# A two-stage transformer block on one core: the first modulation's shift and scale computed by TensorE instead of VectorE

## The chip, the cores and the metric

The kernel runs as one program on one core of a Trainium2 chip. The metric is device time in microseconds from one launch. Three runs of the kernel before gave 3837.38, 3837.87 and 3838.32 us, median 3837.87 us. The engines are PE (TensorE), DVE (VectorE), ACT (ScalarE), POOL (GpSimd) and SP (SyncE, which here only issues transfers). Each runs its own list of instructions in order.

## The reference, cut to what matters

The first lines of the reference make a layer norm of the input, a SiLU of the conditioning vector c, and from it the modulation vectors of every sub-layer. The input of the first feed-forward layer is the normed input, scaled and shifted:

```python
x = layer_norm(x, ln_in_g, ln_in_b)
c_act = jax.nn.silu(c)                       # 1 x 1024
for l in range(DEPTH):
    mod = (c_act @ ada_w[l] + ada_b[l]).reshape(b, N_SUB, 3, 1, D_MODEL)
    h = modulate(x, mod[:, 0, 0], mod[:, 0, 1])   # x * (1 + scale) + shift
    y = swiglu_ffn(h, ffn1_w_in[l], ffn1_w_out[l])
    ...
```

The shift and the scale of the very first `modulate` are two products of a vector of 1024 with a 1024 x 1024 matrix. They stand at the start of the program: no token can enter the first feed-forward layer before its shift and scale are there.

## The kernel before, in words

Everything is float32. Weights and activations are split into a high and a low float32r half (`hi`, `lo`; `hh`, `hl`), and each product is three matmuls (hi.hi, hi.lo, lo.hi: lines 347 to 349). Tokens lie 128 to a partition block (`z`, four blocks of 128 tokens x 1024 features, two blocks in each of two tiles); activations for the matmuls lie with features on the partitions, in eight blocks j = 0 to 7 of 128 features (`h`).

`first_norm` (lines 482 to 531) is the start. DVE sums the rows of z, ACT squares them with an accumulated sum (line 561), DVE and POOL make the reciprocal root, DVE normalizes z in place (line 571, four instructions). Then, for each feature block j, DVE multiplies two fetched weight blocks of 128 x 1024 by the row of SiLU(c), which lies replicated on all partitions (`crow`), with the sum accumulated into one column: one instruction for the shift (line 517), one for the scale (line 518). Four small DVE instructions (lines 519 to 522) fold in the biases and the norm's own gain and bias into `md_in`. PE transposes the block of z (line 525, four 128 x 128 transposes), ACT applies scale and bias on the way out of PSUM (line 528, into `sg` or `gf`) and writes the high half `hh` (line 529), DVE writes the low half `hl` (line 530).

The first chunk of the first feed-forward layer follows directly: gate and up products into the PSUM tiles `pgu`, with 256 tokens at a time, 216 matmuls. They read `hh` and `hl` of the feature blocks in turn, so they start while later blocks are still being made.

All weights come over one transfer queue that SP issues in order: the input, the constant columns `cols`, the 16 blocks of the first modulation (`arawf`, 512 KB each, in a pool of four tiles of two blocks), the first feed-forward weights (`raw`), and blocks of later modulations (`araw`), which DVE multiplies in the same way beside the matmuls (line 463). `gb` holds rows that DVE needs to form the next residual base (lines 594 and 596), also at the start.

The program is written in one order and a scheduler places the instructions on each engine's list by its own timing model, so a change in `first_norm` also moves neighbours that the diff does not touch.

Of the kernel before, what the change touches and what calls it, by code (L numbers as in the profile page):

```python
# [10 lines left out]
F32 = mybir.dt.float32  # L11
F32R = mybir.dt.float32r
AF = mybir.ActivationFunctionType
ALU = mybir.AluOpType
# [3 lines left out]
P = 128  # L18
DM = 1024
KT = DM // P  # L20
# [35 lines left out]
def in_blocks(w):  # L56

    k, m = w.shape
    return w.reshape(k // P, P, m // P, P).transpose(2, 1, 0, 3).reshape(m // P, P, k)
# [65 lines left out]
def mla_uq(w):  # L125
    a, b = [], []
    for g in range(4):
        c = w[:, g * 384 : g * 384 + 384]
        a.append(tok_blocks(c[:256], 2)[0])
        b.append(c[256:])  # L130
    return np.stack(a), np.stack(b)
# [13 lines left out]
def ada_blocks(w):  # L145

    d, _, m = w.shape
    return w.reshape(d, DM, m // DM, KT, P).transpose(0, 2, 3, 4, 1)


def feat(x):
    return x.T.reshape(-1, P, x.shape[0])


def tok(x):

    return x.reshape(-1, 2, P, DM).transpose(0, 2, 1, 3).reshape(-1, P, 2 * DM)


def norm_rows(i):  # L160

    r = [(i["ln_in_g"], i["ln_in_b"])]
    r += [(i["ln_g"][l, s], i["ln_b"][l, s]) for l in range(DEPTH) for s in range(3)]
    r += [(i["ln_g_2"][l, s], i["ln_b_2"][l, s]) for l in range(DEPTH) for s in range(2)]
    r = np.array(r, dtype=np.float32)
    return np.broadcast_to(r[:, :, None], (len(r), 2, P, DM))
# [47 lines left out]

def pack(i):
    c = Cols()
    c.vec("ln_in_g", i["ln_in_g"])
    c.vec("ln_in_b", i["ln_in_b"])
    for l in range(DEPTH):
        for s in range(3):  # L220
            c.vec(f"ln_g{l}{s}", i["ln_g"][l, s])
            c.vec(f"ln_b{l}{s}", i["ln_b"][l, s])
        for s in range(2):
            c.vec(f"ln2_g{l}{s}", i["ln_g_2"][l, s])
            c.vec(f"ln2_b{l}{s}", i["ln_b_2"][l, s])
        c.vec(f"ada_b{l}", i["ada_b"][l])
        c.vec(f"ada2_b{l}", i["b_ada_2"][l])
        for k in range(4):
            c.vec(f"conv_w{l}{k}", i["ssd_conv_w"][l, k])
        c.vec(f"conv_b{l}", i["ssd_conv_b"][l])  # L230
        for k in range(3):
            c.vec(f"sconv_w{l}{k}", i["sconv_w"][l, k])
        c.vec(f"norm_g{l}", i["ssd_norm_g"][l])
        c.vec(f"d{l}", np.repeat(i["ssd_d"][l], 64))
        c.row(f"dtf_b{l}", np.concatenate([i["ssd_dt_bias"][l], i["fox_f_bias"][l]]))
        c.row(f"a_log{l}", i["ssd_a_log"][l])
    c.vec("mla_qg", i["mla_q_norm_2"][0])
    c.vec("mla_kvg", i["mla_kv_norm_2"][0])
    consts, coff = shape_consts()
    uqa, uqb = mla_uq(i["mla_w_uq_2"][0])  # L240
    m_in = i["mla_w_in_2"][0]
    arrays = {
        "x": tok(i["x"][0]),
        "ctx": tok(i["ctx_2"][0]),
        "rows": norm_rows(i),
        "gqa_g": np.broadcast_to(np.concatenate([np.tile(i["gqa_q_norm_2"][0], 4), i["gqa_k_norm_2"][0]]), (P, 320)),
        "ctxT": feat(i["ctx_2"][0]),
        "cols": np.concatenate(c.parts, axis=1),
        "crow": np.stack([np.broadcast_to(v, (P, DM)) for v in (i["c"][0], i["c_2"][0], i["c_ctx_2"])]),
        "consts": consts,  # L250
        "ada": ada_blocks(i["ada_w"]),
        "ada2": ada_blocks(i["w_ada_2"]),
        "f1i": np.stack([ffn_in(w) for w in i["ffn1_w_in"]]),
        "f1o": np.stack([ffn_out(w) for w in i["ffn1_w_out"]]),
        "f2i": np.stack([ffn_in(w) for w in i["ffn2_w_in"]]),
        "f2o": np.stack([ffn_out(w) for w in i["ffn2_w_out"]]),
        "mi": np.stack([mix_in(w) for w in i["mix_w_in"]]),
        "mdt": np.stack([mix_dtf(w) for w in i["mix_w_in"]]),
        "mo": np.stack([mix_out(w) for w in i["mix_w_out"]]),
        "qkv": gqa_in(i["gqa_w_qkv_2"][0]),  # L260
        "gwo": chunks_out(i["gqa_w_o_2"][0]),
        "mcq": tok_blocks(m_in[:, :384], 2),
        "mck": tok_blocks(m_in[:, 384:], KT)[0],
        "uqa": uqa,
        "uqb": uqb,
        "ukv": mla_ukv(i["mla_w_ukv_2"][0]),
        "mwo": chunks_out(i["mla_w_o_2"][0]),
        "w1": np.stack([in_blocks(w) for w in i["mlp_w1_2"]]),
        "w2": np.stack([chunks_out(w) for w in i["mlp_w2_2"]]),
    }  # L270
    return {k: np.ascontiguousarray(v) for k, v in arrays.items()}, c.off, coff
# [40 lines left out]
class Kernel:  # L312
# [171 lines left out]
    def first_norm(self, z, g, b, src, bias):  # L484

        nc, fp = self.nc, self.fpool
        tt, stt, ts = nc.vector.tensor_tensor, nc.vector.scalar_tensor_tensor, nc.vector.tensor_scalar  # L490
        T = lambda tag: fp.tile([P, SEQ], F32, tag=tag, bufs=2, name=tag)
        row = self.vector(0)
        h = self.quads(2, SEQ, "h")
        raw = []

        def fetch(j):
            raw.append(fp.tile([P, 2, DM], F32, tag="q4", bufs=4, name="arawf"))
            for i in range(2):
                nc.sync.dma_start(raw[j][:, i], src[i][j])

        for j in range(4):
            fetch(j)
        md = self.cpool.tile([P, 2, KT], F32, name="md_in")
        acc = self.cpool.tile([P, 3, KT], F32, name="acc_in")
        hs, hb = (md[:, i] for i in range(2))
        sums = self.cpool.tile([P, NTB, 2], F32, name="sums_in")
        for tb in range(NTB):
            for n in range(2):
                x = z[tb // 2][:, tb % 2, n * SEQ : (n + 1) * SEQ]
                nc.vector.tensor_reduce(sums[:, tb, n : n + 1], x, axis=AX, op=ALU.add)  # L510
        self.normalize(z, sums, range(NTB), 1e-5)
        for j in range(KT):
            if j >= 4:
                fetch(j)
            c = lambda x: x[:, j : j + 1]
            m = self.apool.tile([P, DM], F32, tag="amul", bufs=1, name="amul")
            stt(m, raw[j][:, 0], 1.0, row, op0=ALU.mult, op1=ALU.mult, accum_out=c(acc[:, 0]))
            stt(m, raw[j][:, 1], 1.0, row, op0=ALU.mult, op1=ALU.mult, accum_out=c(acc[:, 2]))
            ts(c(acc[:, 2]), c(acc[:, 2]), c(bias[1]), 1.0, op0=ALU.add, op1=ALU.add)
            tt(c(acc[:, 1]), c(acc[:, 0]), c(bias[0]), op=ALU.add)  # L520
            tt(c(hs), c(g), c(acc[:, 2]), op=ALU.mult)
            stt(c(hb), c(b), c(acc[:, 2]), c(acc[:, 1]), op0=ALU.mult, op1=ALU.add)
            pt = self.ps("cd"[j % 2], [P, NTB, P], "pth")
            for tb in range(NTB):
                nc.tensor.transpose(pt[:, tb], z[tb // 2][:, tb % 2, j * P : (j + 1) * P], self.ident)
            hf = T(("sg", "gf")[j % 2])
            hh, hl = (x[:, j % 4] for x in h[j // 4])
            nc.scalar.activation(hf, pt.rearrange("p a e -> p (a e)"), AF.Identity, bias=c(hb), scale=c(hs))
            nc.scalar.copy(hh, hf)
            self.base = tt(hl, hf, hh.bitcast(F32), op=ALU.subtract)  # L530
        return h
# [1123 lines left out]
    def run(self):  # L1655
        nc, tc, d = self.nc, self.tc, self.d
        with ExitStack() as es:
# [8 lines left out]
            z = self.load_rows(d["x"], "z")  # L1666
# [91 lines left out]

            phase("start", True)
            g, b = self.col("ln_in_g", KT), self.col("ln_in_b", KT)  # L1760
            h = self.first_norm(z, g, b, (d["ada"][0, 0], d["ada"][0, 1]), [self.col("ada_b0", KT, i * KT) for i in range(2)])
            later(ada1, 0, 0, (2,))
            for l in range(DEPTH):
                m1 = lambda s, j: mod1[:, l * 9 + s * 3 + j]
# [10 lines left out]
                h = norm(z, self.sums[0], SEQ, 1 + l * 3, m1(1, 0), m1(1, 1), 1e-5, f"md{l}0")  # L1775
                phase(f"mix.{l}", False)
                old, z, kept = z, [], []
# [25 lines left out]
                h = norm(z, self.sums[0], SEQ, 2 + l * 3, m1(2, 0), m1(2, 1), 1e-5, f"md{l}1")  # L1803
# [11 lines left out]
                if l == 0:  # L1815
                    h = norm(z, self.sums[0], SEQ, 3, mod1[:, 9], mod1[:, 10], 1e-5, f"md{l}2")
# [5 lines left out]
            h = norm(z, self.sums[0], SEQ, 6, mod2[:, 0], mod2[:, 1], 1e-5, "md12")  # L1822
            for l in range(DEPTH):
                m2 = lambda j: mod2[:, l * 6 + j]
                kept = keep(z)
                src = self.mla_latents(h, hc) if l else (h, hc, self.gqa_first(hc))
                phase(f"attn.{l}", False)
                z, zc = [], []
# [35 lines left out]
                h = norm(z, sums[-1], SEQ, 7 + 2 * l, m2(3), m2(4), 1e-6, f"me{l}0")  # L1864
                parts = [(h, z, m2(5), SEQ), *more]
                self.mlp(parts, self.base_rows(7 + 2 * l))
                if l == 0:
                    sums = self.sums
                    h = norm(z, sums[0], SEQ, 8, mod2[:, 6], mod2[:, 7], 1e-6, f"me{l}1")
# [30 lines left out]
```

## Time and profile before

| | us |
|---|---|
| median of three runs | 3837.87 |
| profiled execution, its own time | 3839.17 |
| its span, first to last instruction | 3837.3 |
| PE busy | 3637.5 (95%) |
| DVE busy | 2529.1 (66%) |
| ACT busy | 1534.4 (40%) |

A row of the page or of a view gives a line of the kernel, an engine, an operation and its tiles as out<-in. In a view by stretches each engine's busy time stands with its number of instructions, then the granted TensorE clock (1.00 is full speed), the mean busy share of the 16 DMA engines and what they moved. "PEld" is the loading of a matmul's stationary operand. A row of the timeline that stands for several instructions (x8) gives the time from the first's start to the last's end. The granted clock reads 1.00 in the first stretches of this trace, ahead of its first record; there the distance between matmuls shows the level.

### The profile page before, as it was taken

To read this page: it belongs to the slowest core of one execution; us is meant where nothing else is said; L and a number is where in the kernel's file an instruction comes from. 1 tells how busy PE (TensorE), PEld (TensorE's weight loads), DVE (VectorE), ACT (ScalarE), POOL (GpSimd) and SP (SyncE) were. 2 spreads that over 40 slices of the span, in tenths; PEclk is the share of its full clock that TensorE was granted. 3 is DMA by queue.
4 is the path that set the end of the run, shared out by engine and by line. 5 is a ranking of instruction groups with operands and counts; after the bars stand their busy time and mean duration, and the time that the engine had idled before them with its cause. 6 is when DMAs were issued, how large, how long until landed. Compare 5 with 4: busy or idle time off the path is not lost. (4 is left out here: it accounts for less than half of the span.)

```text
span 3837.3 us, 49056 instructions
## 1 busy us (share of the span) xinstructions
PE 3637.5 (95%) x18970; PEld 3077.3 (80%) x18970; DVE 2529.1 (66%) x4245; ACT 1534.4 (40%) x2748; POOL 359.3 (9%) x388
## 2 busy tenths in 40 slices
PE   6999999999999999999998898999999979989998
PEld 5888777888888887778887787788888878878887
DVE  8775665777777966579665778664444558776454
ACT  3222443422332234452224566443232457644333
POOL 0000323000000004310001115100000001130000
PEclk9999999999999999999999899999999989999999
DMA  7663322566446633235642001122221210112222
GB/s 289 213 195 119 106 71 99 167 206 208 158 160 198 208 105 111 71 122 186 208 154 72 21 23 67 35 61 66 66 62 55 77 37 30 41 55 91 95 94 66
DMA packets 121738, 428.77 MB, mean 112 GB/s; under 512 B 13656, under 2 KB 19672, under 8 KB 119072
## 3 DMA queue, kind: packets, MB, share of 16 engines
q1 hardware_dynamic: 119584, 421.44, 33.7%
q10 hardware_dynamic: 1920, 4.19, 0.3%
q8 instruction: 149, 2.44, 0.3%
q14 instruction: 85, 0.70, 0.1%
HBM read 415.10 MB, written 10.49 MB: 111 GB/s over the span
## 5 line engine op out<-in xcount | busy, mean ns | idle before, releaser
L296 ACT CAST hi<-raw 128x1024 fp32r<-128x1024 f32 (+2 forms) x502 | 518.4, 1035 | 1314.4 <-PE pgu L348 726.6
L301 DVE TENSOR_TENSOR lo<-raw,hi 128x1024 fp32r<-128x1024 f32 (+2 forms) x472 | 577.0, 1224 | 337.5 <-ACT hi L296 333.8
L348 PE MATMUL pgu<-hl,hi 128*128 128x512 f32 (+1 forms) x1536 | 567.7, 370 | 4.5 <-DVE hl L530 2.9
L347 PE MATMUL pgu<-hh,hi 128*128 128x512 f32 (+1 forms) x1536 | 565.8, 370 | 5.7 <-ACT hh L621 3.3
L349 PE MATMUL pgu<-hh,lo 128*128 128x512 f32 (+1 forms) x1536 | 566.4, 369 | 0.0
L652 DVE TENSOR_TENSOR po<-po,gate 128x512 f32<-128x512 f32 x376 | 259.0, 696 | 357.6 <-PE po L349 357.6
L347 PE MATMUL po<-hi,gh 128*128 128x512 f32 x1216 | 474.4, 391 | 5.6 <-DVE z L654 3.1
L348 PE MATMUL po<-lo,gh 128*128 128x512 f32 x1216 | 472.8, 390 | 0.0
L349 PE MATMUL po<-hi,gl 128*128 128x512 f32 x1216 | 468.0, 389 | 0.0
L463 DVE SCALAR_TENSOR_TENSOR amul<-araw,crow 128x1024 f32<-128x1024 f32 x288 | 351.4, 1220 | 31.5 <-DMA araw<-in_ada 30.1
L348 PEld LDWEIGHTS pgu<-hl,hi 128*128 128x128 f32 x1536 | 292.8, 191 | 54.0 <-DVE hl L530 3.5
L347 PEld LDWEIGHTS pgu<-hh,hi 128*128 128x128 f32 x1536 | 291.4, 191 | 54.2 <-ACT hh L621 3.7
L349 PEld LDWEIGHTS pgu<-hh,lo 128*128 128x128 f32 x1536 | 292.9, 191 | 47.6 <-DVE lo L301 0.3
L347 PEld LDWEIGHTS po<-hi,gh 128*128 128x128 f32 x1216 | 228.4, 188 | 55.3 <-DVE z L654 5.6
L349 PEld LDWEIGHTS po<-hi,gl 128*128 128x128 f32 x1216 | 228.2, 188 | 47.8
L348 PEld LDWEIGHTS po<-lo,gh 128*128 128x128 f32 x1216 | 228.5, 188 | 45.1
L564 POOL TENSOR_TENSOR st<-st,mhalf 128x2 f32<-128x2 f32 (+2 forms) x24 | 19.9, 828 | 2601.9 <-DVE st L563 2601.9
L348 PE MATMUL pm<-hl,hi 128*128 128x512 f32 (+1 forms) x576 | 210.2, 366 | 2.0 <-DVE hl L622 2.0
L347 PE MATMUL pm<-hh,hi 128*128 128x512 f32 (+1 forms) x576 | 210.3, 367 | 1.9 <-ACT hh L621 1.6
L654 DVE TENSOR_TENSOR z<-po,z 128x512 f32<-128x512 f32 x304 | 206.5, 687 | 5.1
L349 PE MATMUL pm<-hh,lo 128*128 128x512 f32 (+1 forms) x576 | 209.5, 364 | 0.2 <-DVE lo L301 0.2
L333 DVE TENSOR_TENSOR gl<-gf,gh 128x512 fp32r<-128x512 f32 (+1 forms) x158 | 105.3, 668 | 115.7 <-ACT gh L331 115.0
(468 smaller groups left out, 7090.9 us busy)
## 6 DMA issues: line engine op xcount, KB each, us to landing
araw<-in_ada SPq DMA_DIRECT2D x224, 512.0 KB, 4.4
raw<-in_w SPq DMA_DIRECT2D x128, 512.0 KB, 3.5
raw<-in_f1i SPq DMA_DIRECT2D x88, 512.0 KB, 4.2
raw<-in_f2i SPq DMA_DIRECT2D x88, 512.0 KB, 3.8
raw<-in_mi SPq DMA_DIRECT2D x48, 512.0 KB, 3.5
raw<-in_f1o SPq DMA_DIRECT2D x44, 512.0 KB, 4.2
raw<-in_f2o SPq DMA_DIRECT2D x44, 512.0 KB, 4.4
arawf<-in_ada SPq DMA_DIRECT2D x16, 512.0 KB, 9.0
```

What stands on the lines that cost most here:

```text
L296: nc.scalar.copy(hi[:, :n], raw[:, :n])
L301: self.lo = nc.vector.tensor_tensor(lo[:, :n], raw[:, :n], hi[:, :n].bitcast(F32), op=ALU.subtract)
L333: ins = eng.tensor_tensor(lo, src, hi.bitcast(F32), op=ALU.subtract)
L347: mm(ps, ah, bh, start=start and i == 0, stop=False)
L348: mm(ps, ah, bl, start=False, stop=False)
L349: mm(ps, al, bh, start=False, stop=stop and i == n - 1)
L463: ins = nc.vector.scalar_tensor_tensor(m, w, 1.0, row, op0=ALU.mult, op1=ALU.mult, accum_out=res[:, j : j + 1])
L564: nc.gpsimd.tensor_tensor(r, sq, self.mhalf[:, :n], op=ALU.pow)
L652: nc.vector.tensor_tensor(ps, ps, gate[:, f], op=ALU.mult)
L654: nc.vector.tensor_tensor(to, ps, zf, op=ALU.add)
```

## The change

The 16 weight blocks are laid out anew ahead of the launch, with the input features on the partitions (`ada_in`), and c becomes one more set of eight columns in `cols`. The transfers are as many and as large as before. ACT makes SiLU(c) of a 128 x 8 column tile `c_in`. For each feature block j and each of shift and scale, PE does eight float32 matmuls: a 128 x 128 piece of the weights is the stationary operand, one column of `c_in` is the moving one, and they accumulate into one column of the PSUM tile `pmd`. That is 128 matmuls. After every second block DVE folds in biases, gain and bias, two columns at a time, in five small instructions. The transposes and what follows them stand in a loop of their own. The long DVE instructions of lines 517 and 518 are gone. The replicated row `crow` is still loaded, for the later modulations.

```diff
 def pack(i):
     c = Cols()
+    c.vec("c", i["c"][0])
...
+        "ada_in": in_blocks(i["ada_w"][0][:, : 2 * DM]).reshape(2, KT, P, DM),
...
-        row = self.vector(0)
...
-                nc.sync.dma_start(raw[j][:, i], src[i][j])
+                nc.sync.dma_start(raw[j][:, i], src[i, j])
...
-        acc = self.cpool.tile([P, 3, KT], F32, name="acc_in")
+        acc = self.cpool.tile([P, 2, KT], F32, name="acc_in")
+        cv = self.cpool.tile([P, KT], F32, name="c_in")
+        self.silu = nc.scalar.activation(cv, self.col("c", KT), AF.Silu)
+        pm = self.ps("a", [P, 2, KT], "pmd")
...
         for j in range(KT):
             if j >= 4:
                 fetch(j)
-            c = lambda x: x[:, j : j + 1]
-            m = self.apool.tile([P, DM], F32, tag="amul", bufs=1, name="amul")
-            stt(m, raw[j][:, 0], 1.0, row, op0=ALU.mult, op1=ALU.mult, accum_out=c(acc[:, 0]))
-            stt(m, raw[j][:, 1], 1.0, row, op0=ALU.mult, op1=ALU.mult, accum_out=c(acc[:, 2]))
-            ts(c(acc[:, 2]), c(acc[:, 2]), c(bias[1]), 1.0, op0=ALU.add, op1=ALU.add)
-            tt(c(acc[:, 1]), c(acc[:, 0]), c(bias[0]), op=ALU.add)
-            tt(c(hs), c(g), c(acc[:, 2]), op=ALU.mult)
-            stt(c(hb), c(b), c(acc[:, 2]), c(acc[:, 1]), op0=ALU.mult, op1=ALU.add)
+            for i in range(2):
+                for k in range(KT):
+                    w = raw[j][:, i, k * P : (k + 1) * P]
+                    nc.tensor.matmul(pm[:, i, j : j + 1], w, cv[:, k : k + 1], start=k == 0, stop=k == KT - 1)
+            if j % 2:
+                c = lambda x: x[:, j - 1 : j + 1]
+                stt(c(acc[:, 1]), c(pm[:, 1]), 1.0, c(bias[1]), op0=ALU.add, op1=ALU.add)
+                tt(c(acc[:, 0]), c(pm[:, 0]), c(bias[0]), op=ALU.add)
+                tt(c(hs), c(g), c(acc[:, 1]), op=ALU.mult)
+                tt(c(hb), c(b), c(acc[:, 1]), op=ALU.mult)
+                tt(c(hb), c(hb), c(acc[:, 0]), op=ALU.add)
+        c = lambda x: x[:, j : j + 1]
+        for j in range(KT):
             pt = self.ps("cd"[j % 2], [P, NTB, P], "pth")
             ...
```

PE's list at the start of the program. Before, it begins with the transposes of the first four feature blocks (`pth`), and the first gate and up matmuls come between them:

```order
L525 MATMUL pth_185<-ident_75,z_69 128x128 x2
L525 MATMUL pth_185<-ident_75,z_70 128x128 x2
L525 MATMUL pth_201<-ident_75,z_69 128x128 x2
L525 MATMUL pth_201<-ident_75,z_70 128x128 x2
L347 MATMUL pgu_368<-hh_97,hi_291 128x256
L348 MATMUL pgu_368<-hl_98,hi_291 128x256
```

After, the same list begins with the matmuls of two feature blocks into `pmd` (the weight tiles `arawf` are numbered), then the transposes of these two, then the next two, and so on:

```order
L522 MATMUL pmd_114<-c_in_112,arawf_98 128x1 x16
L522 MATMUL pmd_114<-c_in_112,arawf_101 128x1 x16
L534 MATMUL pth_306<-ident_75,z_69 128x128 x2
L534 MATMUL pth_306<-ident_75,z_70 128x128 x2
L534 MATMUL pth_315<-ident_75,z_69 128x128 x2
L534 MATMUL pth_315<-ident_75,z_70 128x128 x2
L522 MATMUL pmd_114<-c_in_112,arawf_104 128x1 x16
L522 MATMUL pmd_114<-c_in_112,arawf_107 128x1 x16
```

So PE gets four groups of 32 one-column matmuls, each ahead of eight transposes; between the second and the third group, and between the third and the fourth, stand twelve gate and up matmuls.

DVE's list at the end of `first_norm`, before (feature blocks 6 and 7, then a multiplication of a later modulation, then the residual base of both tiles of z):

```order
L530 TENSOR_TENSOR hl_100<-sg_263,hh_99 128x512
L530 TENSOR_TENSOR hl_100<-gf_282,hh_99 128x512
L463 SCALAR_TENSOR_TENSOR amul_324,mod1_85<-araw_320,crow_94 128x1024
L594 SCALAR_TENSOR_TENSOR z_69<-z_69,gb_286 128x1024 x2
L594 SCALAR_TENSOR_TENSOR z_70<-z_70,gb_286 128x1024 x2
```

After (lines 603 and 605 are lines 594 and 596 of the kernel before, line 539 is line 530):

```order
L603 SCALAR_TENSOR_TENSOR z_69<-z_69,gb_378 128x1024 x2
L605 SCALAR_TENSOR_TENSOR z_69<-gb_378,z_69 128x1024
L539 TENSOR_TENSOR hl_97<-sg_365,hh_96 128x512
L605 SCALAR_TENSOR_TENSOR z_69<-gb_378,z_69 128x1024
L539 TENSOR_TENSOR hl_97<-gf_374,hh_96 128x512
L465 SCALAR_TENSOR_TENSOR amul_419,mod1_85<-araw_415,crow_412 128x1024
```

The residual base of the first tile of z, four long instructions, now stands ahead of or between the last two low halves; it overwrites z, so it waits for the last transposes of that tile.

## Rows read from the trace of the kernel before

**Rows 1.** The page, engines: busy us, share of the span, instructions.

```profile
PE 3637.5 (95%) x18970; PEld 3077.3 (80%) x18970; DVE 2529.1 (66%) x4245; ACT 1534.4 (40%) x2748; POOL 359.3 (9%) x388
```

**Rows 2.** Stretches of the start: busy time by engine, granted clock, DMA.

```profile
core 0: us, PE busy (x) PEld busy (x) DVE busy (x) ACT busy (x) POOL busy (x), PEclk, DMA share, GB/s
20.00:30.00 10.00, 7.59 (x26) 4.88 (x27) 9.96 (x24) 6.22 (x9) 0.00 (x0) 1.00 1.03 420
30.00:40.00 10.00, 6.46 (x30) 5.44 (x29) 10.00 (x25) 3.07 (x5) 0.00 (x0) 1.00 1.03 420
40.00:50.00 10.00, 5.51 (x23) 4.86 (x23) 9.04 (x21) 5.97 (x8) 0.00 (x0) 0.68 0.44 160
50.00:100.00 50.00, 50.00 (x287) 44.75 (x288) 44.11 (x61) 14.09 (x18) 0.00 (x0) 0.96 0.69 229
350.00:400.00 50.00, 50.00 (x267) 43.32 (x266) 22.62 (x35) 11.71 (x17) 0.00 (x0) 1.00 0.24 74
```

**Rows 3.** PE's first wait: us in total, times, longest.

```profile
PE pth L525 <- DVE z L571: 21.0, 1, 21.0
```

**Rows 4.** PE's timeline at the start: start us, us, engine, line, tiles.

```profile
24.61 1.97 PE L525 MATMUL pth<-ident,z 128*128 128x128 f32 x8 [0.72 <-ACT sg L528]
...
30.16 0.41 PE L347 MATMUL pgu<-hh,hi 128*128 128x256 f32 x1
30.37 0.41 PE L348 MATMUL pgu<-hl,hi 128*128 128x256 f32 x1
...
38.11 0.66 PE L525 MATMUL pth<-ident,z 128*128 128x128 f32 x4 [1.91 <-ACT sg L528]
...
49.92 0.58 PE L348 MATMUL pgu<-hl,hi 128*128 128x256 f32 x1
```

**Rows 5.** The two long DVE instructions: duration ns min/median/max, first and last start.

```profile
L517 DVE SCALAR_TENSOR_TENSOR amul<-arawf,crow x8: 1214/1217/1222, 12.2 to 42.4; 128x1024 f32<-128x1024 f32 x8
...
L594 DVE SCALAR_TENSOR_TENSOR z<-z,gb x4: 1217/1218/1220, 50.9 to 54.3; 128x1024 f32<-128x1024 f32 x4
```

**Rows 6.** Timeline of the start, other engines.

```profile
1.16 1.28 ACT L449 ACT_TABLE_LOAD   x1 [1.16 <-PEq L1889]
...
7.30 1.06 ACT L449 ACTIVATE crow<-crow 128x1024 f32<-128x1024 f32 x1 [4.85 <-DMA crow<-in_crow]
...
10.88 1.13 ACT L561 ACTIVATE junk<-z,st 128x1024 bf16<-128x1024 f32 x1
...
13.62 1.15 ACT L561 ACTIVATE junk<-z,st 128x1024 bf16<-128x1024 f32 x1
...
15.15 2.04 POOL L564 TENSOR_TENSOR st<-st,mhalf 128x4 f32<-128x4 f32 x1 [14.72 <-DVE st L563]
...
20.18 2.97 DVE L571 TENSOR_SCALAR z<-z,st 128x1024 f32<-128x1024 f32 x4
...
49.17 0.69 DVE L530 TENSOR_TENSOR hl<-gf,hh 128x512 fp32r<-128x512 f32 x1 [0.95 <-ACT hh L529]
```

**Rows 7.** A float32 matmul with 32 moving columns: its loads and matmuls.

```profile
L931 PEld LDWEIGHTS pdec<-a,mstrict x4: 188/190/192, 488.4 to 1496.7; 128*128 128x128 f32 x4
```

**Rows 8.** Weight loads in order of time, at full clock.

```profile
488.79 0.30 PEld L932 LDWEIGHTS pdec<-a,tri 128*128 128x128 f32 x2
489.01 0.19 PEld L348 LDWEIGHTS pqk<-hl,hi 128*128 128x128 f32 x1
```

**Rows 9.** Weight loads of four transposes at the start.

```profile
38.11 0.42 PEld L525 LDWEIGHTS pth<-ident,z 128*128 128x128 f32 x4 [2.20 <-ACT sg L528]
```

**Rows 10.** The page, transfers: count, KB each, median us to landing.

```profile
arawf<-in_ada SPq DMA_DIRECT2D x16, 512.0 KB, 9.0
```

**Rows 11.** Granted clock in stretches of 2 us around the end of the start.

```profile
44.00:46.00 2.00, 0.00 (x0) 0.00 (x0) 2.00 (x4) 2.00 (x3) 0.00 (x0) 1.00 0.00 0
...
50.00:52.00 2.00, 2.00 (x9) 2.00 (x10) 2.00 (x3) 0.00 (x0) 0.00 (x0) 0.50 0.53 199
...
54.00:56.00 2.00, 2.00 (x19) 2.00 (x18) 2.00 (x3) 0.00 (x0) 0.00 (x0) 1.00 0.03 10
```

**Rows 12.** The longest total of PE's waits within attention.

```profile
PE ptt L1221 <- DVE pt L333: 16.7, 21, 3.9
```

More of the change, by code (lines that the diff above doesn't have):

```diff
@@ L1760, in run @@
             g, b = self.col("ln_in_g", KT), self.col("ln_in_b", KT)
-            h = self.first_norm(z, g, b, (d["ada"][0, 0], d["ada"][0, 1]), [self.col("ada_b0", KT, i * KT) for i in range(2)])
+            h = self.first_norm(z, g, b, d["ada_in"], [self.col("ada_b0", KT, i * KT) for i in range(2)])
             later(ada1, 0, 0, (2,))
```

## The prediction

> **What bounds the kernel now.** I read the page's engine totals first, then stretches, then the timeline and waits of the start. PE is busy 95% of the span [rows 1], and from 50 to 400 us it has no gap at all: the stretches show 50.00 of 50.00 us [rows 2]. What delays PE's entry into that stretch delays the end by as much, and work taken from DVE behind 50 us is worth nothing. So the case is decided in the first 50 us. There PE waits 21.0 us for the first normalized z [rows 3] and is then busy 7.59, 6.46 and 5.51 us in each 10, while DVE is busy 9.96 and 10.00 us of 20 to 40 and 9.04 of 40 to 50 [rows 2]: DVE is the bound of the start, and the 16 long multiplications are most of it. The transfer queue is full as well, 420 GB/s until 40 us [rows 2].
>
> As a mark I take the gate-and-up matmul that waits for the last low half `hl` of feature block 7. By both orders 44 such matmuls stand ahead of it. It starts at 49.92 us before [rows 4], and PE never waits from there to 400 us. Where it starts after the change is the forecast.
>
> **What the change removes.** On DVE: 16 instructions of 1.22 us, 19.5 us [rows 5], and some 8 us of small ones; their replacements are 20 of a fifth of a us. That takes DVE off the path, as long as PE has something ready.
>
> **What ACT and the norm do.** SiLU(c) now stands behind the second Square, which ends at 12.0 us (10.88 + 1.13), and needs a table load of 1.28 us [rows 6]; with some 0.3 us for eight columns and the semaphore (an estimate, under the 1.06 us that 1024 columns take) the first matmul can start at 13.7 us. The SiLU of `crow` now stands ahead of the third Square, so the Squares end at about 17.3 us where they ended at 14.9 (13.62 + 1.15 and the read). POOL's 2.04 us and three small DVE steps follow, and the four normalizations (2.97 us) run from 20.3 to 23.3 us. Before they ran from 20.18 to 23.15 [rows 6], because long multiplications stood between. So this is even.
>
> **What PE gets.** 128 one-column matmuls. A plain float32 matmul is two loads and two passes: line 931 is one matmul in each of two layers and shows four loads [rows 7]. So 256 passes. A column of moving data is nearly nothing; the load of 128 x 128 sets the pace. At full clock loads follow each other every 0.11 us (two in 0.30, each 0.19 long; the third 0.22 after the first [rows 8]): 28.2 us. At half clock the 256-column matmuls, whose array time equals such a load's, are 0.21 us apart at 30 us [rows 4]: 0.213, so 54.5 us. The only cheaper rows are loads for transposes, four in 0.42 us, one per 0.09 [rows 9]. These are the ends: 0.09 to 0.213, none below nothing, since each load occupies PE's one loading path. Before, PE did about 19 us of work ahead of the mark and waited the rest; at least 23 us come on top, and nothing hides them but these waits.
>
> Which level? The first stretches lie at half speed (1.2 GHz): matmuls 0.21 us apart at 30 us [rows 4], while 54 to 56 us has 19 of the same in 2 us [rows 11]. At 50 to 52 us the granted clock is 0.50 although PE is busy throughout, and by 54 us, after four us of back-to-back 256-column matmuls, it is 1.00 [rows 11]. Every rise at the start follows such a run; no row shows a run of loads with one-column matmuls. I take half clock for these, the nearest row by place, and keep full clock as a rival.
>
> The sum at half clock: A, start 13.7 us, two blocks, 64 passes x 0.213 = 13.6, to 27.3. Eight transposes at 1.97 / 8 = 0.25 [rows 4], to 29.3; z is ready. 64 passes, to 42.9; transposes, to 44.9; twelve matmuls x 0.213 = 2.6, to 47.5. 64 passes, to 61.1; transposes and twelve, to 65.7. 64 passes, to 79.3; transposes, to 81.3. Then DVE's new order: the residual base of z's first tile waits for the transposes (about 80.7), and two of 1.22, one of 1.22, `hl` of block 6 (0.69), one of 1.22 and `hl` of block 7 (0.69) stand in a row [rows 5, 6]: 6.3 us, the mark at 87.0. PE's last 20 matmuls (4.3 us) lie beside it. That is 37 us later.
>
> From this goes a part: the two runs of transposes and matmuls (4.6 us each, at 42.9 and 61.1) may lift the clock for a while behind them. In the trace it was 1.00 at 44 to 46 us, after such a run, and 0.50 again at 50 [rows 11]. A lift of 3 us saves about 3 us of passes. I take half of two, 3 us: 34 us later. Past the mark the clock has to rise anew as before (even, within 2 us).
>
> Transfers do not bind: a block of 512 KB [rows 10] takes 1.25 us at 420 GB/s, and the last modulation block, behind 15.9 MB, can land at 42 us; at half clock its tile is free only at 42.9 (its predecessor is read by then), so it lands near 45.5, and is needed at 72. SP's waits for PE hold back feed-forward weights in the queue too, but those land by 46 us and their chunk's continuous run starts at 87.
>
> The profiled run took 3839.17 us, 1.3 more than the median of the runs. 3839.2 + 34 = 3873; against the median, **3872 us**.
>
> **Rivals.**
> *Full clock.* If loads alone count as work for the clock, it rises some 4 us after 13.7 us (it took 4 us from 49.92 to 54). A then ends at 22.7, the transposes with the last z at 24.5, and DVE frees the columns at 24.9; three times 64 x 0.11 = 7.0 and transposes of 1.3 (0.66 for four [rows 4]), with twice twelve matmuls of 1.4 between, give 52.6; DVE's 6.3 us from half a us earlier, the mark at 58.4. That is 8.5 us later, 3846 us. For it: PE is without a gap. Against: no row of that kind. The Trainium skill, TensorE: Matmul & The Clock Gate, "What's actually happening", has the clock gate opened by how busy the engine has been; read literally this stream is busy, and by that rule this rival holds. No row here shows whether loads count.
> *Not slower: passes cheaper than the rows.* If a pass took under about 0.07 us, PE would no longer be the bound. From 24.5 us, 192 passes, 3.9 us of transposes and 2.8 of matmuls would end by 43.8, and the last block, landed at 42.2 us, would set the end: its passes and transposes to 44.0, DVE's 6.3 us, the mark at 50.3, 3838 us. For it only that moving data are 128 times fewer than in any row; against it the 0.11 us at 32 columns, itself set by the load [rows 7, 8]. The same page, "Wait — 56ns, not 53.3ns?", gives a floor of about 25 ns between matmuls however small; an estimate by that alone is 6.4 us for all passes, and this rival's time. It speaks of matmuls without their loads; the trace's 0.11 decides against it.
> *Faster by the scheduler.* The order also moves rows in the last latent attention, where PE waits for DVE: the largest total of such waits is 16.7 us over 21 waits, the longest 3.9 [rows 12]. A moved wait or two is 4 us either way, too little to turn the sign of the others. So even the best start (0 to 1 us) plus this gives 3834.
>
> **How the numbers follow.** Half clock 65%, full clock 25%, cheap passes 7%, an outcome turned by the scheduler 3%. About 0.2% (7.7 us) can be told from no change. Half clock's own range is 3860 to 3879 (more lifts below; none, and 2 us of clock, above). The range reaches to the full clock: 3845 to 3879. Slower: all of half clock and two thirds of full clock, 82%. Same: the rest of full clock and most of the cheap passes, 14%. Faster: 4%.
>
> **What would show it.** In the new trace: 256 loads on line 522, with a pace of 0.21 us (right), 0.11 (full clock) or under 0.07; PE's first instruction at 13.7 us; the normalizations at 20 to 23 us; the granted clock low through the four groups; DVE idle most of 25 to 80 us; the mark near 84 us and no gap behind it. It is wrong if the clock is 1.00 inside the groups, if PE waits there for blocks or for ACT, or if the mark is right and the end is not later by as much: then a later wait took it up.

## The result, and the profile after

The changed kernel takes 3867.8 us (median of 4 runs, 3866.7 to 3868.7) against 3838.1 us before; the ratio is 1.0075, 95% interval 1.0062 to 1.0089. It is slower by 29.7 us; 34 were forecast, and the time lies inside the forecast range of 3845 to 3879. The profiled execution took 3868.73 us with a span of 3866.9.

The engine totals of the page after (busy us, share of the span, instructions) answer to [rows 1]:

```profile
PE 3688.7 (95%) x19226; PEld 3130.1 (81%) x19226; DVE 2507.6 (65%) x4201; ACT 1536.1 (40%) x2750; POOL 358.3 (9%) x388
```

PE has 51.2 us and 256 records more, DVE 21.5 us less: the work went over as forecast, at a worse price. The stretches of the start after, in the columns of [rows 2], show which engine bounds it now:

```profile
20.00:30.00 10.00, 10.00 (x49) 10.00 (x49) 5.43 (x11) 4.10 (x5) 0.00 (x0) 1.00 1.02 403
40.00:50.00 10.00, 10.00 (x63) 10.00 (x63) 1.97 (x7) 2.70 (x4) 0.00 (x0) 0.96 0.57 211
60.00:70.00 10.00, 10.00 (x49) 10.00 (x49) 1.11 (x2) 0.99 (x2) 0.00 (x0) 0.50 0.00 0
80.00:90.00 10.00, 8.80 (x71) 8.60 (x72) 10.00 (x12) 0.00 (x0) 0.00 (x0) 1.00 0.34 107
```

In the three tens shown from 20 to 70 us PE is full. DVE, 9 to 10 us busy in each 10 from 20 to 50 before, is busy 5.4 us in the first of them and 2 or less in the other two. The timeline of PE after answers to [rows 4] (start us, us, engine, line, tiles; in brackets the idle time before and what ended it):

```profile
13.44 13.81 PE L522 MATMUL pmd<-c_in,arawf 128*128 128x1 f32 x64 [13.44 <-ACT c_in L507]
27.11 1.95 PE L534 MATMUL pth<-ident,z 128*128 128x128 f32 x8
28.85 13.65 PE L522 MATMUL pmd<-c_in,arawf 128*128 128x1 f32 x64
42.37 1.95 PE L534 MATMUL pth<-ident,z 128*128 128x128 f32 x8
...
46.25 11.02 PE L522 MATMUL pmd<-c_in,arawf 128*128 128x1 f32 x64
57.13 1.95 PE L534 MATMUL pth<-ident,z 128*128 128x128 f32 x8
...
61.44 13.65 PE L522 MATMUL pmd<-c_in,arawf 128*128 128x1 f32 x64
74.94 1.95 PE L534 MATMUL pth<-ident,z 128*128 128x128 f32 x8
...
80.44 0.39 PE L350 MATMUL pgu<-hl,hi 128*128 128x256 f32 x1 [0.56 <-DVE hl L539]
...
82.18 0.39 PE L350 MATMUL pgu<-hl,hi 128*128 128x256 f32 x1 [0.75 <-DVE hl L539]
```

Four groups of 64 passes stand one behind the other; from one group's start to the next instruction are 13.67, 13.52, 10.88 and 13.50 us. The mark, the last row, is at 82.18 us, 32.3 us later than in [rows 4]. The first float32 matmul of line 940 (line 931 in [rows 7], whose first load is at 488.4) tells how much of that is left 440 us on. In the row of its loads the durations stand first, then the first and the last start:

```profile
L940 PEld LDWEIGHTS pdec<-a,mstrict x4: 188/190/192, 519.0 to 1529.4; 128*128 128x128 f32 x4
```

It is 30.6 us later, and the end of the span 29.6.

### The profile page after: what moved, and what is told of

It reads as the page before. It is cut to its first block, busy times and chain, and to the rows that moved or that the text cites. A ratio compares the mean times of both kernels' runs of the same rounds, so it can differ in the third digit from the quotient of the medians.

```text
span 3866.9 us, 49515 instructions
## 1 busy us (share of the span) xinstructions
PE 3688.7 (95%) x19226; PEld 3130.1 (81%) x19226; DVE 2507.6 (65%) x4201; ACT 1536.1 (40%) x2750; POOL 358.3 (9%) x388
```

## The experiments

Every kernel below was timed against the kernel before on the same chip. As a common measure I use the time at which the last low half `hl` of the first norm is ready (start plus duration of its row on DVE), since the mark waits for it.

| kernel | last low half ready, us | span, us | median, us | ratio to before (95%) |
|---|---|---|---|---|
| before | 49.9 | 3837.3 | 3838.1 | |
| after | 82.1 | 3866.9 | 3867.8 | 1.0075 (1.0062 to 1.0089) |
| 128 columns | 59.0 | 3848.4 | 3850.9 | 1.0033 (1.0021 to 1.0045) |
| half the products | 55.0 | 3841.4 | 3844.6 | 1.0013 (1.0004 to 1.0022) |
| an eighth | 46.9 | 3833.8 | 3836.5 | 0.9996 (0.9987 to 1.0005) |
| order | 76.7 | 3864.6 | 3865.8 | 1.0071 (1.0058 to 1.0084) |
| 128 columns and order | 55.4 | 3839.8 | 3841.4 | 1.0005 (0.9996 to 1.0014) |
| block 0 on PE | 51.2 | 3839.9 | 3839.8 | 1.0007 (0.9998 to 1.0016) |
| blocks 0, 1 on PE, 128 columns | 47.7 | 3832.8 | 3840.5 | 0.9999 (0.9990 to 1.0008) |
| blocks 0, 1 on PE, one column | 50.3 | 3846.9 | 3848.1 | 1.0018 (1.0009 to 1.0027) |

The second and third columns are of one profiled execution each. The span less the second column lies between 3784.4 and 3789.4 us in nine of the ten kernels: what the start loses, the end loses, to within 5 us. A difference of less than that between two starts cannot be read from the end. The last kernel is told of below.

**1. The same loads, 128 moving columns.** The theory is half clock; its strongest rival is that the loads take 0.213 us by themselves. The products, the loads and the result stay; the moving operand is wider, so `pmd` becomes one tile for every two blocks, of which DVE reads one column for each product:

```diff
-        pm = self.ps("a", [P, 2, KT], "pmd")
...
+            if j % 2 == 0:
+                pm = self.ps("a", [P, 2, 2, P], "pmd")
...
-                    nc.tensor.matmul(pm[:, i, j : j + 1], w, cv[:, k : k + 1], start=k == 0, stop=k == KT - 1)
+                    nc.tensor.matmul(pm[:, i, j % 2], w, cv[:, k : k + 1].broadcast_to([P, P]), start=k == 0, stop=k == KT - 1)
...
```

The scheduler lays the lists out anew with it: PE has 128 passes in a row at its start, ahead of the first transposes. Its first 64 passes stand as in the changed kernel.

> The same 128 products with the same 256 weight loads, but the moving operand is the column of SiLU(c) repeated to 128 columns, so that each pass also has 128 columns of array work; the result is the same. Theory A (the clock stays at half speed through the one-column groups because one-column matmuls do not lift it): with the wider moving operand the granted clock rises early in the groups, a pass then takes about 0.11 us instead of 0.213, three or four groups of 64 end 6 to 6.6 us earlier each, the mark (the gate-and-up matmul waiting for the last low half of feature block 7) comes at about 58 to 63 us instead of 82.2, and the time is 3845 to 3850 us. Rival B (the weight loads set 0.213 us whatever the moving operand, or the clock is held down by something else): pace and clock as in the changed kernel, 3868 us, 128 columns at half clock hiding beside the load. Rival C (the wider pass costs more array time than the load): slower than 3868.

It took 3850.9 us, 16.9 less than the changed kernel: 0.9 above theory A's range, and B falls. The weight loads of the line (duration ns min/median/max) in this kernel, and below them those of the changed kernel:

```profile
L523 PEld LDWEIGHTS pmd<-c_in,arawf x256: 187/191/338, 13.5 to 50.3; 128*128 128x128 f32 x128
```

```profile
L522 PEld LDWEIGHTS pmd<-c_in,arawf x256: 187/333/337, 13.4 to 74.7; 128*128 128x128 f32 x128
```

The same load has a median of 191 ns here and 333 there. The stretches of 2 us of this kernel's start show where it turns (the count behind PE is what to read; the granted clock stands at 1.00 in this column from the start, as it does at 30 us in the kernel before, where matmuls are 0.21 us apart, so up to the first change only the pace tells the level):

```profile
14.00:16.00 2.00, 2.00 (x11) 2.00 (x11) 0.00 (x0) 2.00 (x4) 0.00 (x0) 1.00 1.03 412
16.00:18.00 2.00, 2.00 (x17) 2.00 (x16) 0.17 (x1) 0.69 (x2) 1.01 (x1) 1.00 1.02 408
18.00:20.00 2.00, 2.00 (x20) 2.00 (x20) 1.88 (x5) 0.00 (x0) 0.00 (x0) 1.00 1.03 412
```

Eleven passes in 2 us, then 17, then 20: some 3 us from its start at 13.54 PE has doubled its pace. With one column it stays at 11 or 12 in each stretch up to 46 us. Behind the first rise the recorded clock can be read too. The changed kernel at 46 to 82 us:

```profile
46.00:48.00 2.00, 2.00 (x21) 2.00 (x19) 0.69 (x1) 0.26 (x1) 0.00 (x0) 1.00 0.31 123
48.00:50.00 2.00, 2.00 (x16) 2.00 (x16) 0.00 (x0) 0.00 (x0) 0.00 (x0) 0.78 0.00 0
50.00:52.00 2.00, 2.00 (x11) 2.00 (x11) 0.00 (x0) 0.00 (x0) 0.00 (x0) 0.50 0.27 31
...
76.00:78.00 2.00, 2.00 (x12) 2.00 (x11) 1.71 (x2) 1.89 (x3) 0.00 (x0) 0.50 0.00 0
...
80.00:82.00 2.00, 0.98 (x6) 0.78 (x6) 2.00 (x3) 0.00 (x0) 0.00 (x0) 1.00 0.00 0
```

The clock, at 1.00 behind the run of matmuls that ends at 46.25, falls to 0.50 at 49 us inside the third group, with PE busy 2.00 of every 2 us, and comes back near 80. This speaks against the reading on which the rival of full clock rested (the Trainium skill, TensorE: Matmul & The Clock Gate, "What's actually happening": how busy the engine has been sets the gate): by PE's busy share in the profile the two kernels are alike, and their clocks are not. The pace of the wide passes, 7.31 us for the 64 from 36.38 us, is 0.114 us each, so at full clock the load still sets it, as in [rows 8].

What then held this kernel is on DVE (timeline, columns as for PE):

```profile
50.68 0.16 DVE L526 SCALAR_TENSOR_TENSOR acc_in<-pmd,cols 128x2 f32<-128x2 f32 x1 [4.36 <-PE pmd L523]
...
50.82 2.35 DVE L604 SCALAR_TENSOR_TENSOR z<-z,gb 128x1024 f32<-128x1024 f32 x2
...
53.23 2.35 DVE L606 SCALAR_TENSOR_TENSOR z<-gb,z 128x1024 f32<-128x1024 f32 x2
55.50 0.15 DVE L530 TENSOR_TENSOR md_in<-md_in,acc_in 128x2 f32<-128x2 f32 x1
```

```profile
57.75 0.80 PE L349 MATMUL pgu<-hh,hi 128*128 128x256 f32 x2 [5.36 <-ACT hh L539]
```

The last step of shift and scale, 0.15 us long, stands behind four long instructions of the residual base, and PE idles 5.36 us.

**2. Half the products.** The loop over the pieces of c ends at 4 of 8:

```diff
-                for k in range(KT):
+                for k in range(4):
...
-                    nc.tensor.matmul(pm[:, i, j : j + 1], w, cv[:, k : k + 1], start=k == 0, stop=k == KT - 1)
+                    nc.tensor.matmul(pm[:, i, j : j + 1], w, cv[:, k : k + 1], start=k == 0, stop=k == 3)
```

> Leaves out half of the products of shift and scale (4 of the 8 pieces of c), so 64 matmuls and 128 weight loads remain. Theory A (the passes are the cost, in a row on the path of the start): 128 passes less at 0.17 to 0.213 us, 22 to 27 us, so the mark at 55 to 60 us instead of 82.2 and 3841 to 3846 us. Rival D (what moved the mark is VectorE's new order ahead of the last low halves, or blocks that land late): the time stays above 3855.

3844.6 us, with the low half at 55.0: theory A. D falls: the four of the residual base still stand ahead of and between the last two low halves, as in the changed kernel, and the time went down by 23.3 us. The low half comes 27.1 us earlier, 0.21 us for each of the 128 passes left out; by the time it is 0.18. The two need not agree: the passes that are left do not all run at half clock (16 of them take 1.84 us from 37.30), and PE waits 2.76 and 1.16 us ahead of its last low halves.

**3. An eighth of the products**, by the same edit (`range(1)`): what is left if the passes cost next to nothing.

> Leaves out 7 of 8 products of shift and scale: 16 matmuls and 32 weight loads remain, so VectorE is relieved of the long multiplications and TensorE has next to nothing in their place. It shows what the start could gain at best from taking the multiplications off VectorE. Theory A: the passes take under 7 us in all, TensorE is not the bound; the last modulation block, landing near 42 us, then sets the end with VectorE's 6 us of residual base and low halves behind it: mark 46 to 51 us, 3835 to 3840 us, no real gain over before. Rival E (VectorE was the only bound): the mark 10 us or more ahead of 49.9, 3828 us or less.

3836.5 us, theory A; the interval includes no change. Its reason was only partly right. PE's timeline in this kernel:

```profile
40.88 0.42 PE L522 MATMUL pmd<-c_in,arawf 128*128 128x1 f32 x2
45.00 0.79 PE L349 MATMUL pgu<-hh,hi 128*128 128x256 f32 x2 [3.70 <-ACT hh L538]
46.35 0.58 PE L350 MATMUL pgu<-hl,hi 128*128 128x256 f32 x1 [0.55 <-DVE hl L539]
```

PE waits for no transfer before its last two passes at 40.88; they stand behind other matmuls in its own order. Behind them 6 us of DVE, ACT and DVE lead to the last low half, and these no form of the products removes. The residual base, which theory A put among them, stands behind the last low half in this kernel, at 47.95. So 3.0 us on the low half, 1.7 us (0.04%) on the time, is about all that taking the multiplications off DVE could give in this order of work.

**4. DVE's old order.** The residual base is held behind the last low half, in the changed kernel (`turns` is 0 in the first norm alone):

```diff
+        self.turns = getattr(self, "turns", -1) + 1
...
-                self.after(ins, self.normed if tb < t // P // 2 else self.base)
+                self.after(ins, self.normed if tb < t // P // 2 and self.turns else self.base)
```

> All of the change, with VectorE's residual base of the first normalization held behind the last low half, as before the change, so that nothing long stands between the last transposes and the last two low halves. Theory A (the weight passes on TensorE are the cost; VectorE's order only adds the end): the waits of 0.56 and 0.75 us for low halves go and the mark comes about 1 to 2 us earlier, 80.5 to 81.2 us, time 3866 to 3867 us, not to be told from 3868. Rival D (VectorE's order costs the 6.3 us of the sum): mark near 76.5, 3862 us.

3865.8 us, 2.0 less: theory A by the time, and the two intervals overlap. The fourth group and DVE's last low half in this kernel:

```profile
61.29 10.94 PE L522 MATMUL pmd<-c_in,arawf 128*128 128x1 f32 x64
```

```profile
76.00 0.69 DVE L539 TENSOR_TENSOR hl<-gf,hh 128x512 fp32r<-128x512 f32 x1 [0.64 <-ACT hh L538]
```

The low half is ready at 76.7, 5.4 us earlier, near the 76.5 where rival D put the mark. But that is partly luck: the clock was up at the start of the fourth group here (1.00 at 62 to 64 us, 0.50 in the changed kernel), the group took 10.8 us instead of 13.5, and the transposes behind it start 2.85 us earlier. DVE's order gives the other 2.6. The mark comes at 78.0, 4.2 us earlier, between the two readings: 2.85 are the clock's, and 1.3 are the two waits for low halves, 0.56 and 0.75, which are gone, since PE has matmuls left when the low half is ready. So of the 6.3 us of rival D's sum 1.3 are on PE's path, and the 2.0 us of time are no measure of DVE's order.

**5. Both edits, 128 columns and DVE's old order.**

> The 128-column moving operand and, with it, the residual base of the first normalization held behind the last low half. With the wide operand alone TensorE ran dry at 52.4 us and waited 5.4 us for the last high half, because on VectorE 4.7 us of residual base and a transfer-bound step stood between the last read of the products (50.7) and the last step of shift and scale (55.5). Theory A2 (at full clock the passes no longer decide alone, VectorE's order does): the last high and low halves come at 53 to 55 us instead of 57.1 to 59, the mark at 53.5 to 55 us instead of 58.5, and the time is 3844 to 3847 us, 4 us better than the wide operand alone and still slower than before, since the passes themselves hold PE until 52 us. Rival (the wait is for something else, such as the last block's landing): no change against the wide operand alone, 3851 us.

3841.4 us, 9.5 less than with 128 columns alone; more than either reading said. PE and DVE in this kernel:

```profile
54.12 0.51 PE L349 MATMUL pgu<-hh,hi 128*128 128x256 f32 x2 [1.01 <-ACT hh L539]
54.85 0.39 PE L350 MATMUL pgu<-hl,hi 128*128 128x256 f32 x1 [0.22 <-DVE hl L540]
```

```profile
54.71 0.69 DVE L540 TENSOR_TENSOR hl<-gf,hh 128x512 fp32r<-128x512 f32 x1
...
56.45 4.63 DVE L605 SCALAR_TENSOR_TENSOR z<-z,gb 128x1024 f32<-128x1024 f32 x4
```

The low half comes 3.6 us earlier. The clock adds to it: in the kernel with 128 columns alone it fell from 1.00 to 0.50 during the wait of 5.36 us. The stretch of 50 to 60 us, with 128 columns alone and then with both edits:

```profile
50.00:60.00 10.00, 4.64 (x30) 4.21 (x30) 7.24 (x12) 2.47 (x4) 0.00 (x0) 0.71 0.00 1
```

```profile
50.00:60.00 10.00, 8.77 (x73) 8.36 (x72) 6.49 (x13) 2.47 (x4) 0.00 (x0) 1.00 0.18 52
```

The granted clock is 0.71 there and 1.00 here. The first matmul with 512 moving columns, with 128 columns alone and then with both edits, shows what that is worth:

```profile
78.43 0.50 PE L349 MATMUL pgu<-hh,hi 128*128 128x512 f32 x1
```

```profile
73.43 0.40 PE L349 MATMUL pgu<-hh,hi 128*128 128x512 f32 x1
```

It comes 5.0 us earlier: 3.6 by the low half and 1.4 by the clock. The spans differ by 8.6 us. The other 3.6 arise later, and I have no account of them; the six times with 128 columns alone lie as far apart as 3847.5 and 3856.3. What is left, 3.3 us over before, is inside the interval.

**6. Part of the blocks on PE, the rest on DVE as before.** In the kernel before, block 0, or blocks 0 and 1, take the new form. The edit for two blocks and 128 columns, cut (block 0 alone takes `j < 1` and one column):

```diff
+            if j < 2:
+                ...
+                for i in range(2):
+                    for k in range(KT):
+                        w = raw[j][:, i, k * P : (k + 1) * P]
+                        nc.tensor.matmul(pm[:, i, j], w, cv[:, k : k + 1].broadcast_to([P, P]), start=k == 0, stop=k == KT - 1)
```

> The kernel before, with shift and scale of feature block 0 alone taken by TensorE (32 one-column passes), blocks 1 to 7 on VectorE. TensorE idles until 24.6 us before, waiting for z; 32 passes at half clock, 6.8 us from 13.6, lie inside that wait, and VectorE loses two of 1.22 us. Theory A (passes cost only where they stand on the path, VectorE bounds the start): mark 1.5 to 2.5 us earlier than 49.9, 3835.5 to 3837 us, at most 0.07% under before, not to be told from it. Rival F (the extra table load and SiLU on ScalarE delay the normalization by more than that): 3838 to 3841.

3839.8 us, above theory A's range: a miss, though not to be told from before. Its number is rival F's, its cause is not: z is normalized at 18.47 us, earlier than before. DVE's order again put two of the residual base in front of the last low half:

```profile
48.22 2.35 DVE L608 SCALAR_TENSOR_TENSOR z<-z,gb 128x1024 f32<-128x1024 f32 x2
50.49 0.68 DVE L544 TENSOR_TENSOR hl<-gf,hh 128x512 fp32r<-128x512 f32 x1
```

So this run says little about passes inside PE's wait.

> Feature blocks 0 and 1 by TensorE with the 128-column moving operand (64 passes, clock up after 3 us: 13.6 to 22.3 us, inside the wait for z), blocks 2 to 7 on VectorE, which loses four of 1.22 us, 4.9 us. Theory A: the mark 3 to 4.5 us earlier, bounded by the last block's landing as in the run with an eighth of the products (mark 46.3, 3.6 us earlier): 3833.5 to 3836 us, 0.05 to 0.12% under before. Rival F (ScalarE's extra table load delays the normalization, or the transposes wait for the passes): 3838 or more.

By its median, 3840.5 us, a miss with rival F's number. Yet the low half is ready at 47.7, 2.1 us earlier than before, z is normalized from 16.83 us, and the profiled execution took 3834.6 us. The eleven times fall apart: five lie between 3833.0 and 3835.0, below all 33 of the kernel before (3836.4 to 3841.0), and six between 3840.5 and 3843.2. The median is the lowest of the six. On the whole no difference can be told, and what parts the times I did not find.

> The same with the one-column moving operand: 64 passes at half clock, 13.65 us, end at 27.3, 2.7 us past the point where the transposes started before. Theory A (half clock for one-column passes): TensorE's first transposes come at 27.3 instead of 24.6, so 1 to 4 us worse than the 128-column form, 3835 to 3840 us. Rival B (the moving operand's width is without effect on the clock when the passes stand alone): the same as with 128 columns.

3848.1 us: 7.6 more than with 128 columns, beyond theory A's range, though B falls as before. PE, with one column and then with 128:

```profile
12.23 6.99 PE L526 MATMUL pmd<-c_in,arawf 128*128 128x1 f32 x32 [12.23 <-ACT c_in L508]
...
21.00 6.99 PE L526 MATMUL pmd<-c_in,arawf 128*128 128x1 f32 x32
```

```profile
12.44 5.96 PE L526 MATMUL pmd<-c_in,arawf 128*128 128x128 f32 x32 [12.44 <-ACT c_in L508]
...
21.21 3.84 PE L526 MATMUL pmd<-c_in,arawf 128*128 128x128 f32 x32 [0.90 <-DVE acc_in L528]
```

The second 32 passes take 6.99 us against 3.84: the clock once more. In this pair nothing but the moving operand's width was edited. That and DVE's order make the low half 2.5 us later. The two profiled spans differ by 14.1 us, but they are not alike: the eleven times fall apart here too, five from 3839.2 to 3842.4 and six from 3848.1 to 3851.3, and the profile is one of the six, while that with 128 columns is one of its five short ones. Between short and short, or long and long, the medians differ by about 7 us. Where the part of it beyond the low half arises these two profiles cannot tell.

No version that keeps all products is faster than the kernel before by more than its interval.

## Why the prediction was right

**The bound.** Right: [rows 2] showed PE without a gap from 50 to 400 us, and in nine kernels the time from the last low half to the end is the same within 5 us.

**256 passes at half clock.** Right, and shown by experiments 1 and 2: 256 loads on line 522, 13.5 us for 64, or 0.211 us each (0.213 forecast). The ends of the bounds are seen as well: 0.114 us at full clock with 128 columns. The rival of full clock, with a mark of 58.4 and 3846 us, is near what experiment 1 gives, with its last low half at 59.0 and 3850.9 us: its condition was not met by one column. Its parts met less well than its sum. With 128 columns the last passes end at 50.5, earlier than it had them, and DVE and ACT then take longer than its 6.3 us. That of cheap passes is closed: 128 times fewer columns made no pass cheaper than its load.

**Start, ACT and the norm.** PE began at 13.44 us (13.7). The four normalizations came at 18.51 instead of 20.3: the Squares ended at 16.6 instead of 17.3, and POOL's instruction took 1.01 us where [rows 6] has 2.04. The miss is harmless: z was ready long before the first transposes. The rows after:

```profile
13.18 0.21 ACT L507 ACTIVATE c_in<-cols 128x8 f32<-128x8 f32 x1
...
16.88 1.01 POOL L573 TENSOR_TENSOR st<-st,mhalf 128x4 f32<-128x4 f32 x1 [16.45 <-DVE st L572]
...
18.51 2.98 DVE L580 TENSOR_SCALAR z<-z,st 128x1024 f32<-128x1024 f32 x4
...
76.29 2.36 DVE L603 SCALAR_TENSOR_TENSOR z<-z,gb 128x1024 f32<-128x1024 f32 x2 [0.55 <-PE pth L534]
...
81.44 0.69 DVE L539 TENSOR_TENSOR hl<-gf,hh 128x512 fp32r<-128x512 f32 x1
```

**The lifts of the clock.** Right in the sum by luck, wrong in the parts: I took half of two lifts, 3 us. One run of twelve matmuls, ending at 46.25, lifted it and saved 2.6 us of the third group (10.88 against 13.5); the other, at 58.7 to 61.4, did nothing. In experiment 4, whose start differs by 0.2 us, that one lifted it as well, and the fourth group took 10.8 us. So single lifts of this kind were not mine to forecast; only a half. The first 3 us of the third group are also the one place where the prediction's own sign against half clock, 1.00 inside a group, was seen.

**Transposes and DVE's tail.** Eight transposes cost 1.6 to 1.74 us from their start to the next instruction, not the 1.97 of [rows 4], whose duration overlaps what follows: 1.0 us in the three that are on the path in full. DVE's tail ran from 76.29 to 82.13, 5.8 us (6.3). These and PE's start, 0.26 us early, are the larger part of what brings the mark to 82.18 instead of 84.

**Transfers.** Right: the last modulation block was issued at 42.5 and 42.9 us, when its tile came free, and the fourth group never waited for it.

**Behind the mark.** This step was off: I called the clock's rise there even, within 2 us. The kernel before crossed the mark at half clock and stayed there until 53.7 us; the changed kernel had 1.00 from 79.8 us, before its mark. At 0.213 against 0.12 us for a matmul that is 18 matmuls, 1.7 us, given back. The first matmul with 512 moving columns, before and after, has it:

```profile
69.50 0.40 PE L347 MATMUL pgu<-hh,hi 128*128 128x512 f32 x1
```

```profile
100.02 0.40 PE L349 MATMUL pgu<-hh,hi 128*128 128x512 f32 x1
```

Of the 32.3 us at the mark 30.5 are left there, 30.6 by line 940 and 29.6 at the end. It is read from the traces and was not tried by itself. Of the last 1.0 us I have no account; the spans of the four runs after differ by 2.0. Of the 4.3 us by which the forecast was too long, 1.7 are this step, 1.7 the mark, and the rest is that open end.

**How the 29.7 us divide.** Wide columns take off 16.9, DVE's order then 9.5, and 3.3 are left. They hold for this order of undoing alone. Undone first, DVE's order was worth 1.3 us at the mark (experiment 4), because PE's passes cover what DVE does late; and of the 9.5 only 5.0 are found in the start (experiment 5).

## What to carry to other kernels

Before work is moved to a nearly full engine, look at the one stretch in which that engine starts: a share of 95% over the whole says nothing of where its idle time lies, and what is put ahead of a run without gaps is paid almost in full. Price a one-column float32 matmul by its two weight loads, and at the clock that nearby rows show; when such a stream runs at half clock, the cheapest trial is to repeat the column, which left loads and result alike here and took a pass from 0.211 to 0.114 us. And where an edit frees an engine, check what the scheduler then moves into the freed place: long work that nobody waits for can land in front of the short step that everybody waits for.

## What the runs showed of the hardware

- PE fully busy with one-column float32 matmuls was at half clock in all of the first two groups (11 or 12 in 2 us, 0.211 us each), and from 49 to 79.8 us with transposes and twelve matmuls between; the same loads with 128 columns went from 11 to 20 passes in 2 us some 3 us after the start.
- A wait of 5.36 us of PE was followed by half clock until 61.0 us, so that the wait cost more than the late data: without it the low half came 3.6 us earlier and the first matmul with 512 columns 5.0.
- POOL's power of 128 x 4 elements took 2.04 us before, 1.92 with one block on PE and 1.01 in the other eight kernels; one of DVE's long multiplications ran beside it in the first two and in none of the eight. Whether that is the cause was not tried by itself.
